# A Strassen-type matrix product whose shared products are handed from PSUM bank to PSUM bank

## The chip, the core and the metric

The kernel runs on one core of a Trainium2 chip: TensorE (PE) multiplies matrices into PSUM, VectorE (DVE) and ScalarE (ACT) work on SBUF and PSUM, GpSimd (POOL) does a little, and SyncE (SP) issues the weight transfers. The metric is the device time of one execution in microseconds, as the median of several runs. The profile comes from one execution more.

## What is computed

One block of a hybrid encoder, fp32, on 256 tokens of width 2048:

```python
def mixer_block(u, w_in, lb, hg_norm_w, rel_bias, w_branch_a, w_branch_b, w_out):
    z = u @ w_in
    hq, hf, hi, hg, aq, ak, av, gates = jnp.split(z, SPLIT_POINTS, axis=-1)
    ...
    o = hgrn2_scan(...)                              # 8 heads, chunks of 64
    y_a = rms_norm(o, hg_norm_w) * silu(hg)
    y_b = chunk_band_attention(aq, ak, av, rel_bias) # 16 heads
    gate_a, gate_b = jnp.split(jax.nn.sigmoid(gates), 2, axis=-1)
    merged = gate_a * (y_a @ w_branch_a) + gate_b * (y_b @ w_branch_b)
    return merged @ w_out

h = x + mixer_block(rms_norm(x, norm_mix_w), ...)
u = rms_norm(h, norm_mlp_w)
h = h + jnp.square(jax.nn.relu(u @ w_up)) @ w_down   # 2048 -> 8192 -> 2048
return rms_norm(h, norm_final_w)
```

`w_in` is 2048 x 11264, its last 4096 columns are the gates.

## The kernel before

**Products in three parts.** Each fp32 operand is split into a high part in the PE's fast fp32 format and the remainder (`split`, L88: a cast on ACT, a subtraction on DVE), and each product is three matmuls, high by high, high by low, low by high (`mm3`, L142). All weights pass through this: a piece is 128 x 1024 (two k-tiles of 512 columns, 512 KB), read by a DMA that SP issues into one of 7 raw buffers, cast on ACT (`wh`, 6 buffers), subtracted on DVE (`wl`, 6 buffers), then used by 12 matmuls of 512 columns, six for each half m of the tokens.

**Order of the stages.** The start and the HGRN2 projections and scan (`hf`, `hq`, `hi`, `hg`), attention (`aq`, `ak`, `av`), the first two column blocks of gate a (`gemm`, L150), then everything else in units of two column blocks (`gemm_s`, L680): ga2, gb0, gb2 (gates), the two branch products (`gemm2`, plain), wo0 and wo2 (output projection), and for each quarter q of the MLP up q0, up q2, dn q0, dn q2. These are 20 units; the very last, dn32, is a plain product by `gemm2`.

**A unit.** Of its 16 k-tiles the k-tiles 0, 1, 4, 5 form a 2 x 2 block problem (halves m of the tokens, halves n of the columns, two blocks of k), done with seven products p1 to p7 instead of eight, six matmuls each. The left operands of four of them are sums of blocks (S5, S2, S4, S7), made once for each left matrix by `combos` (L659): two full sums, four differences and four splits. The right operands are sums of weight pieces, made in place by `add` on DVE (L693). The other twelve pieces are `plain` (L715), 12 matmuls each, so a unit has 7 x 6 + 12 x 12 = 186 matmuls. Four banks c11, c12, c21, c22 collect the outputs. Products that belong to several outputs are copied on ACT from PSUM to SBUF (`copy`, L703: s1 of p1, s5 of p5, s6 of p6, s67 of p6 + p7), combined on DVE after the tenth k-tile (L746 to L748; for units whose result is added to the residual h1, also with h1 by `fold`, L751), and added or subtracted when the banks are evicted on DVE (`evict`, L654). Gates then take a sigmoid on ACT (L582), up units ReLU (L874) and square (L875).

**What sets the order.** The kernel is written as a sequence, and a scheduler places every instruction on its engine's queue; `high_priority` moves instructions ahead. The pools set what a buffer waits for: PSUM has six banks in `ps_k` for units and two in `ps_tp2` for transposes. The sums of x for the gates (`Sx`, L755) are made at the start of ga2, with the highest priority; those for the other stages inside earlier units. Transposes and splits of the finished blocks (`turn`, `turns`) run between products of the following unit (`between`), those of the last up blocks ahead of the down unit (L879).

Of the kernel before, what the change touches and what calls it, by code (L numbers as in the profile page):

```python
# [16 lines left out]
P = 128  # L17
# [33 lines left out]
def tile_hybrid_block(  # L51
# [205 lines left out]
    mask1 = const.tile([P, 64], F32, name="mask1")  # L257
    band(mask1, [[-2, 64]], 1)
    masks = const.tile([P, len(LEVELS), 192], F32, name="masks")
# [4 lines left out]
    reset = const.tile([P, 2 * T], F32, name="reset")  # L264
    nc.gpsimd.memset(reset, 1.0)
    nc.gpsimd.memset(reset.rearrange("p (c t) -> p c t", t=CH)[:, :, 0:1], 0.0)
    hgw = const.tile([P, DK], F32, name="hgw")
# [233 lines left out]
    yb = []  # L501

# [73 lines left out]
    def token(what):  # L576
        return tk.tile([P, NC], F32, name=what, tag="t", bufs=18)
# [6 lines left out]

    ga, gb = [], []
# [68 lines left out]
    def evict(dst, acc, t, op):  # L654
        with tc.high_priority(offset=2000):
            nc.vector.tensor_tensor(dst, acc, t, op=op)
        return dst

    def combos(lhs, what, home):  # L659

        full = []
        for j in range(2):
            f = tk.tile([P, 2, T], F32, name=f"full_{what}{j}", tag="t", bufs=18)
            nc.vector.tensor_tensor(f, lhs[j][:, :2, 0, :].bitcast(F32), lhs[j][:, :2, 1, :].bitcast(F32), op=ALU.add)
            full.append(f)
        a11, a21 = full[0][:, :, :P], full[0][:, :, P:]
        a12, a22 = full[1][:, :, :P], full[1][:, :, P:]
        made = {}
        s = {i: tk.tile([P, 2, P], F32, name=f"s{i}_{what}", tag="t", bufs=18) for i in (5, 2, 4, 7)}
        nc.vector.tensor_tensor(s[5], a21, a22, op=ALU.subtract)  # L670
        nc.vector.tensor_tensor(s[2], s[5], a11, op=ALU.subtract)
        nc.vector.tensor_tensor(s[4], a12, s[2], op=ALU.add)
        nc.vector.tensor_tensor(s[7], a11, a21, op=ALU.subtract)
        for i in (4, 2, 7, 5):
            t = xp.tile([P, 2, 2, P], F32R, name=f"S{i}_{what}", tag=f"S{i}{home}", bufs=1)
            split(t[:, :, 0, :], t[:, :, 1, :], s[i])
            made[i] = t
        return made

    def gemm_s(lhs, S, w, n0, what, kt0=0, between=None, fold=None):  # L680

        n1 = n0 + NC
        c = {}
        B = {}
        for i, (n, k) in {"11": (n0, 0), "22": (n1, 4), "12": (n1, 0), "21": (n0, 4)}.items():
            B[i] = piece(w, n, kt0 + k, f"{what}{i}")

        def add(dst, b):
            with tc.high_priority(offset=2000):
                nc.vector.tensor_tensor(B[dst], B[dst], B[b], op=ALU.add)  # L693

        def product(i, lh, src, n):
            first = i not in c
            if first:
                c[i] = bank(f"{what}c{i}")
            wh, wl = parts(B[src], w, f"{what}{n}")
            for a in range(2):  # L700
                mm3(c[i], *lh(a), wh[:, a], wl[:, a], first and a == 0, False)

        def copy(i, n):  # L703
            t = token(f"{n}_{what}")
            with tc.high_priority(offset=2000):
                nc.scalar.copy(t, c[i])
            return t

        def of(m, jj):
            return lambda k: lhs_of(lhs, k + 4 * jj, m)  # L710

        def comb(i):
            return lambda k: [S[i][:, k, u, :] for u in range(2)]

        def plain(k, n):  # L715
            wh, wl = parts(piece(w, n0 + n * NC, kt0 + k, f"{what}r{n}_{k}"), w, f"{what}r{n}_{k}")
            for m in range(NM):
                for a in range(2):
# [12 lines left out]
        f = copy("21", "s6")  # L731
        product("11", of(0, 1), "21", "p2")
        plain(6, 1)
        product("21", comb(7), "22", "p7")
        e = copy("21", "s67")
        add("21", "11")
        product("21", of(1, 1), "21", "p4")
        if between:
            between()
        for k in (2, 6, *range(8, KD, 2)):  # L740
            for n in range(2):
                if n == 0 or k >= 8:
                    plain(k, n)
            if k == 10:
                with tc.high_priority(offset=2000):
                    nc.vector.tensor_tensor(f, f, s5, op=ALU.subtract)  # L746
# [47 lines left out]
    def h_blocks(n0):  # L794

        for n in (n0, n0 + 1):
            hT.append(new_act(f"h{n}"))
            hi, lo = hT[n][:, :, 0, :], hT[n][:, :, 1, :]
            for m in range(NM):
                t = h1[n][m]  # L800
                tp = transpose4(t, f"h{n}{m}")
                tmp = tk.tile([P, 4, P], F32, name=f"hw_{n}_{m}", tag="t", bufs=18)
# [11 lines left out]
    for n0 in (0, 2):  # L814
# [26 lines left out]
    for qd in range(NQ):  # L841
# [23 lines left out]
        for c in range(0, 4, 2):  # L865
            rs = {}
            for m, n, acc, t, op in gemm_s(hT, Sh, w_up, qd * (FF // NQ) + c * NC, f"up{qd}{c}", between=turns):
                z = acc
                if t is None:
                    t = token(f"r{qd}{c}")  # L870
                else:
                    z = evict(t, acc, t, op)
                with tc.high_priority(offset=2000):
                    nc.scalar.activation(t, z, AF.Relu, scale=rstd2[:, m:m + 1])  # L874
# [8 lines left out]
        for n, m, acc, t, op in down(uT, Su, qd, last):  # L883
            r = h1[n][m]
            evict(r, acc, r if t is None else t, op or ALU.add)
            if not last:
                continue
            nc.scalar.activation(token(f"ysq_{n}_{m}"), r, AF.Square, accum_out=ssq3[:, m, n:n + 1])
            if n < 3:
                nc.vector.tensor_tensor(r, r, wf[:, n * NC:(n + 1) * NC], op=ALU.mult)  # L890
                continue
# [3 lines left out]
            for i in range(4):  # L895
# [7 lines left out]
                (nc.sync if i % 2 else nc.scalar).dma_start(out[m * P:(m + 1) * P, i * NC:(i + 1) * NC], t)  # L903

# [43 lines left out]
```

## Time and profile before

| | |
|---|---|
| median of 3 runs | 1459.68 us (1458.53 to 1459.84) |
| profiled execution | 1457.01 us, span 1455.3 us |
| mean granted TensorE clock | 0.995 |
| HBM read and written | 269.57 MB, 2.10 MB: 187 GB/s over the span |
| weight loads (PEld) | 1185.7 us busy, 81% |

The span is the time between the first and the last instruction. PE matmuls overlap, so the distance between two starts says more than a duration: a matmul of 512 columns has a record of 0.39 us while the next starts after 0.23. The page and the queries list an instruction group by line, engine, operation, output and inputs, with the count, and in brackets the idle time of the engine ahead of it and what ended it. The bracket names the event that came last, not all that was waited for. The granted clock is a share of full speed.

### The profile page before, as it was taken

To read this page: it belongs to the slowest core of one execution; us is meant where nothing else is said; L and a number is where in the kernel's file an instruction comes from. 1 tells how busy PE (TensorE), PEld (TensorE's weight loads), DVE (VectorE), ACT (ScalarE), POOL (GpSimd) and SP (SyncE) were. 2 spreads that over 40 slices of the span, in tenths; PEclk is the share of its full clock that TensorE was granted. 3 is DMA by queue.
4 is the path that set the end of the run, shared out by engine and by line. 5 is a ranking of instruction groups with operands and counts; after the bars stand their busy time and mean duration, and the time that the engine had idled before them with its cause. 6 is when DMAs were issued, how large, how long until landed. Compare 5 with 4: busy or idle time off the path is not lost.

```text
span 1455.3 us, 18340 instructions
## 1 busy us (share of the span) xinstructions
PE 1430.2 (98%) x6738; PEld 1185.7 (81%) x6738; DVE 1095.4 (75%) x1444; ACT 812.8 (56%) x1060; POOL 34.5 (2%) x96
## 2 busy tenths in 40 slices
PE   9999999999998999999999999999999999999997
PEld 8878888888786888888888888888888888888886
DVE  7888987565657775678898878878777887778853
ACT  6855743464545554445556565566555664457642
POOL 2000001010000000010000000000000000000000
PEclk9999999999999999999999999999999999999999
DMA  9644554646456556666555576555666555667561
GB/s 319 228 152 143 165 170 137 192 131 188 139 167 214 193 180 217 191 219 216 182 168 166 195 230 201 193 183 162 198 221 217 192 165 170 212 202 247 180 196 58
DMA packets 106091, 272.89 MB, mean 188 GB/s; under 512 B 8960, under 2 KB 9728, under 8 KB 105616
## 3 DMA queue, kind: packets, MB, share of 16 engines
q1 hardware_dynamic: 103264, 264.80, 55.8%
q0 software_dynamic: 1584, 5.31, 1.4%
q10 hardware_dynamic: 1152, 1.60, 0.3%
q8 instruction: 53, 0.87, 0.2%
q14 instruction: 38, 0.31, 0.1%
HBM read 269.57 MB, written 2.10 MB: 187 GB/s over the span
## 4 chain that ended last, share of the span: by engine, by line
PE 90%; DVE 3%; DMA 2%; ACT 2%; issue 1%; POOL 0%; SPq 0%; POOLq 0%; ACTq 0%; DVEq 0%
PE acc_ak L171 2%; PE acc_aq L171 2%; PE acc_hq L171 2%; PE ps L395 1%; PE acc_hf L171 1%; PE acc_ba L145 1%; PE acc_bb L145 1%; PE acc_bb L144 1%; PE acc_av L143 1%; PE acc_av L145 1%; PE acc_ba L144 1%; PE acc_bb L143 1%; PE acc_ba L143 1%; PE acc_av L144 1%; PE acc_up22c L143 1%
## 5 line engine op out<-in xcount | busy, mean ns | idle before, releaser
L171 PE MATMUL acc_hf<-act_x,wh_hf 128*128 128x512 f32 x128 | 47.6, 407 | 0.4 <-DVE f L179 0.4
L171 PE MATMUL acc_aq<-act_x,wh_aq 128*128 128x512 f32 x128 | 47.8, 407 | 0.0
L171 PE MATMUL acc_hq<-act_x,wh_hq 128*128 128x512 f32 x128 | 45.6, 396 | 0.0
L171 PE MATMUL acc_ak<-act_x,wh_ak 128*128 128x512 f32 x128 | 45.0, 397 | 0.0
L693 DVE TENSOR_TENSOR raw_up<-raw_up,raw_up 128x1024 f32<-128x1024 f32 x32 | 39.2, 1225 | 1.1
L170 PE MATMUL acc_aq<-act_x,wl_aq 128*128 128x256 f32 x120 | 35.1, 293 | 0.0
L693 DVE TENSOR_TENSOR raw_dn<-raw_dn,raw_dn 128x1024 f32<-128x1024 f32 x28 | 34.3, 1225 | 1.0
L170 PE MATMUL acc_hf<-act_x,wl_hf 128*128 128x256 f32 x120 | 34.4, 287 | 0.1
L90 DVE TENSOR_TENSOR wl_ga<-raw_ga,wh_ga 128x1024 fp32r<-128x1024 f32 x16 | 19.6, 1224 | 19.5 <-ACT wh_ga L89 19.5
L170 PE MATMUL acc_hq<-act_x,wl_hq 128*128 128x256 f32 x120 | 33.6, 280 | 0.0
L170 PE MATMUL acc_ak<-act_x,wl_ak 128*128 128x256 f32 x120 | 33.6, 280 | 0.0
L90 DVE TENSOR_TENSOR wl_av<-raw_av,wh_av 128x1024 fp32r<-128x1024 f32 x16 | 19.6, 1224 | 18.1 <-ACT wh_av L89 18.1
L90 DVE TENSOR_TENSOR wl_dn<-raw_dn,wh_dn 128x1024 fp32r<-128x1024 f32 x16 | 19.6, 1224 | 16.9 <-ACT wh_dn L89 16.9
L90 DVE TENSOR_TENSOR wl_ba<-raw_ba,wh_ba 128x1024 fp32r<-128x1024 f32 x16 | 19.6, 1225 | 16.3 <-ACT wh_ba L89 16.3
L89 ACT CAST wh_ba<-raw_ba 128x1024 fp32r<-128x1024 f32 x16 | 16.9, 1053 | 24.8 <-PE acc_ba L145 10.0
L90 DVE TENSOR_TENSOR wl_bb<-raw_bb,wh_bb 128x1024 fp32r<-128x1024 f32 x16 | 19.6, 1224 | 13.8 <-ACT wh_bb L89 13.8
L90 DVE TENSOR_TENSOR wl_ak<-raw_ak,wh_ak 128x1024 fp32r<-128x1024 f32 x16 | 19.6, 1224 | 13.7 <-ACT wh_ak L89 13.7
L89 ACT CAST wh_bb<-raw_bb 128x1024 fp32r<-128x1024 f32 x16 | 16.9, 1054 | 23.0 <-PE acc_ba L145 11.7
L89 ACT CAST wh_dn<-raw_dn 128x1024 fp32r<-128x1024 f32 x16 | 16.9, 1054 | 23.0 <-PE acc_dn L145 13.3
L89 ACT CAST wh_av<-raw_av 128x1024 fp32r<-128x1024 f32 x16 | 16.8, 1053 | 22.0 <-PE acc_av L145 12.4
L89 ACT CAST wh_aq<-raw_aq 128x1024 fp32r<-128x1024 f32 x16 | 16.8, 1050 | 21.5 <-PE acc_aq L171 8.1
L171 PEld LDWEIGHTS acc_hf<-act_x,wh_hf 128*128 128x128 f32 x128 | 24.2, 189 | 5.5 <-DVE f L179 0.7
(845 smaller groups left out, 5100.4 us busy)
## 6 DMA issues: line engine op xcount, KB each, us to landing
raw_dn<-in_w_down_dram SPq DMA_DIRECT2D x44, 512.0 KB, 4.5
raw_up<-in_w_up_dram SPq DMA_DIRECT2D x32, 512.0 KB, 5.0
raw_ga<-in_w_in_t_dram SPq DMA_DIRECT2D x20, 512.0 KB, 4.5
raw_hi<-in_w_in_n_dram SPq DMA_DIRECT2D x16, 512.0 KB, 4.5
raw_hg<-in_w_in_n_dram SPq DMA_DIRECT2D x16, 512.0 KB, 3.7
raw_aq<-in_w_in_t_dram SPq DMA_DIRECT2D x16, 512.0 KB, 4.6
raw_ak<-in_w_in_t_dram SPq DMA_DIRECT2D x16, 512.0 KB, 3.8
raw_av<-in_w_in_n_dram SPq DMA_DIRECT2D x16, 512.0 KB, 4.3
```

The costliest lines, as they stand in the source:

```text
L89: (copy or nc.scalar.copy)(hi, src)
L90: nc.vector.tensor_tensor(lo, src, hi.bitcast(F32), op=ALU.subtract)
L143: nc.tensor.matmul(acc, hi, wh, start=first, stop=False, skip_group_check=True)
L144: nc.tensor.matmul(acc, hi, wl, start=False, stop=False, skip_group_check=True)
L145: nc.tensor.matmul(acc, lo, wh, start=False, stop=last, skip_group_check=True)
L170: nc.tensor.matmul(acc[:, cb, 0:T], wl[:, c], r[:, 0, :], start=False, stop=False)
L171: nc.tensor.matmul(acc[:, cb, :], wh[:, c], r.rearrange("p u t -> p (u t)"), start=kt == 0, stop=kt == nkt - 1)
L395: nc.tensor.matmul(ps[:, m, :], klf[:, a * P:(a + 1) * P], qrf[:, a * 192:(a + 1) * 192], start=True, stop=True)
L693: nc.vector.tensor_tensor(B[dst], B[dst], B[b], op=ALU.add)
```

## The change

The unit's schedule of products is another. p1 is copied on ACT from bank c11 into bank c21, and p6 and later p7 accumulate on that copy. After p6 the bank is copied to SBUF as u1; `less` (DVE) writes c12 = c22 − u1, c22 holding p5, and p3 and the plain pieces add onto it. After p7 it is copied as u2, and `less` writes c22 = c22 − u2. All four banks then hold their outputs at the end, so no combining and no folding is left: `done` is called for each bank when it is complete, ReLU and sigmoid read PSUM, and h1 takes one addition per bank as before. The first three banks that are written by ACT or DVE get one matmul of values that are overwritten (`fresh`).

The last plain piece of column half n1 with the two `done` calls after it is kept in `late` and stands in the next unit, between p5 and p6 (`flush`). The sums of x are made in the attention stage, their tiles in the pool `tk`. The transposes ahead of a down unit now stand inside it (`between=turns`). The masks, the reset row and `hgw` move to the pool `hp` (the first of these lines is shown). In the whole program PE gets 3 matmuls more, DVE 80 TENSOR_TENSOR fewer, ACT 20 copies fewer; the DMAs are the same in number.

```diff
@@ -254,17 +254,17 @@
-    mask1 = const.tile([P, 64], F32, name="mask1")
+    mask1 = hp.tile([P, 64], F32, name="mask1")
...
@@ -582,6 +583,28 @@
+    def combos(lhs, what, home):
+        full = []
+        for j in range(2):
+            f = tk.tile([P, 2, T], F32, name=f"full_{what}{j}", tag="t", bufs=TOK)
+            nc.vector.tensor_tensor(f, lhs[j][:, :2, 0, :].bitcast(F32), lhs[j][:, :2, 1, :].bitcast(F32), op=ALU.add)
+            full.append(f)
...
+        for i in (4, 2, 7, 5):
+            t = (tk if home == "a" else xp).tile([P, 2, 2, P], F32R, name=f"S{i}_{what}", tag=f"S{i}{home}", bufs=1)
+            split(t[:, :, 0, :], t[:, :, 1, :], s[i])
+            made[i] = t
+        return made
+    Sx = combos(xT, "x", "a")
     ga, gb = [], []
     for n in range(2):
         acc = gemm(xT, w_in_t, C_GA + n * NC, KD, f"ga{n}", wide=True)
@@ -651,33 +674,11 @@
-    def evict(dst, acc, t, op):
+    def evict(dst, acc):
         with tc.high_priority(offset=2000):
-            nc.vector.tensor_tensor(dst, acc, t, op=op)
+            nc.vector.tensor_tensor(dst, acc, dst, op=ALU.add)
-        return dst
-    def combos(lhs, what, home):
...
-            t = xp.tile([P, 2, 2, P], F32R, name=f"S{i}_{what}", tag=f"S{i}{home}", bufs=1)
...
-    def gemm_s(lhs, S, w, n0, what, kt0=0, between=None, fold=None):
+    def gemm_s(lhs, S, w, n0, what, done, kt0=0, between=None, fresh=()):
@@ -693,18 +694,17 @@
-            first = i not in c
-            if first:
-                c[i] = bank(f"{what}c{i}")
             wh, wl = parts(B[src], w, f"{what}{n}")
-            for a in range(2):
-                mm3(c[i], *lh(a), wh[:, a], wl[:, a], first and a == 0, False)
-        def copy(i, n):
-            t = token(f"{n}_{what}")
-            with tc.high_priority(offset=2000):
-                nc.scalar.copy(t, c[i])
-            return t
+            def mm():
+                first = i not in c
+                if first:
+                    c[i] = bank(f"{what}c{i}")
+                for a in range(2):
+                    mm3(c[i], *lh(a), wh[:, a], wl[:, a], first and a == 0, False)
+            return mm
         def of(m, jj):
             return lambda k: lhs_of(lhs, k + 4 * jj, m)
@@ -714,54 +714,94 @@
         def plain(k, n):
             wh, wl = parts(piece(w, n0 + n * NC, kt0 + k, f"{what}r{n}_{k}"), w, f"{what}r{n}_{k}")
-            for m in range(NM):
+            def mm(m):
                 for a in range(2):
                     mm3(c["12"[m] + "12"[n]], *lhs_of(lhs, k + a, m), wh[:, a], wl[:, a], False, k + a == KD - 1)
-        product("11", of(0, 0), "11", "p1")
-        s1 = copy("11", "s1")
-        product("12", comb(4), "22", "p3")
+            return mm
+        def copy(dst, i):
+            with tc.high_priority(offset=2000):
+                nc.scalar.copy(dst, c[i])
+            return dst
+        def seeded(i):
+            c[i] = bank(f"{what}c{i}")
+            if i in fresh:
+                nc.tensor.matmul(c[i], lhs[0][:, 0, 0, 0:P], lhs[0][:, 0].rearrange("p u t -> p (u t)"), start=True, stop=False, skip_group_check=True)
+        def less(dst, i, t):
+            with tc.high_priority(offset=2000):
+                nc.vector.tensor_tensor(c[dst], c[i], t, op=ALU.subtract)
+        p1 = product("11", of(0, 0), "11", "p1")
+        p3 = product("12", comb(4), "22", "p3")
         add("22", "12")
         add("12", "11")
-        product("22", comb(5), "12", "p5")
-        s5 = copy("22", "s5")
-        plain(2, 1)
+        p1()
+        seeded("21")
+        copy(c["21"], "11")
+        product("22", comb(5), "12", "p5")()
+        flush()
         add("11", "22")
-        product("21", comb(2), "11", "p6")
-        f = copy("21", "s6")
-        product("11", of(0, 1), "21", "p2")
-        plain(6, 1)
-        product("21", comb(7), "22", "p7")
-        e = copy("21", "s67")
+        product("21", comb(2), "11", "p6")()
+        u1 = copy(token(f"u1_{what}"), "21")
+        seeded("12")
+        less("12", "22", u1)
+        product("11", of(0, 1), "21", "p2")()
+        ps = plain(2, 0)
+        ps(0)
+        p3()
+        product("21", comb(7), "22", "p7")()
         add("21", "11")
-        product("21", of(1, 1), "21", "p4")
+        u2 = copy(token(f"u2_{what}"), "21")
+        pq = plain(2, 1)
+        pq(0)
+        pq(1)
+        product("21", of(1, 1), "21", "p4")()
+        less("22", "22", u2)
+        ps(1)
         if between:
             between()
-        for k in (2, 6, *range(8, KD, 2)):
-            for n in range(2):
-                if n == 0 or k >= 8:
-                    plain(k, n)
-            if k == 10:
-                with tc.high_priority(offset=2000):
-                    nc.vector.tensor_tensor(f, f, s5, op=ALU.subtract)
-                    nc.vector.tensor_tensor(f, f, s1, op=ALU.add)
-                    nc.vector.tensor_tensor(e, e, s1, op=ALU.add)
-                    if fold:
-                        for m, n, t, op in ((1, 0, s1, ALU.add), (0, 1, f, ALU.subtract), (1, 1, e, ALU.subtract)):
-                            nc.vector.tensor_tensor(t, t, fold(m, n), op=op)
-        return [(0, 0, c["11"], None, None), (1, 0, c["21"], s1, ALU.add), (0, 1, c["12"], f, ALU.subtract), (1, 1, c["22"], e, ALU.subtract)]
-    with tc.high_priority(offset=4000):
-        Sx = combos(xT, "x", "a")
-    for gates, c, col, what in ((ga, 2, C_GA, "ga"), (gb, 0, C_GB, "gb"), (gb, 2, C_GB, "gb")):
+        def both(n, *ks):
+            for k in ks:
+                ps = plain(k, n)
+                ps(0)
+                ps(1)
+        def end(n):
+            for m in range(NM):
+                done(m, n, c["12"[m] + "12"[n]])
+        both(0, 6, 8)
+        both(1, 6, 8)
+        both(0, 10, 12, 14)
+        end(0)
+        both(1, 10, 12)
+        def rest():
+            both(1, 14)
+            end(1)
+        late.append(rest)
+    late = []
+    def flush():
+        while late:
+            late.pop()()
+    for gates, c, col, what, fresh in ((ga, 2, C_GA, "ga", ("21", "12")), (gb, 0, C_GB, "gb", ("21",)), (gb, 2, C_GB, "gb", ())):
         gates += [[None] * NM for _ in range(2)]
-        for m, n, acc, t, op in gemm_s(xT, Sx, w_in_t, col + c * NC, f"{what}{c}"):
-            z = acc
-            if t is None:
-                t = token(f"gate_{what}{c + n}{m}")
-            else:
-                z = evict(t, acc, t, op)
-            gates[c + n][m] = sigmoid(t, z, m)
+        def done(m, n, acc, gates=gates, c=c, what=what):
+            gates[c + n][m] = sigmoid(token(f"gate_{what}{c + n}{m}"), acc, m)
+        gemm_s(xT, Sx, w_in_t, col + c * NC, f"{what}{c}", done, fresh=fresh)
+    flush()
     mT = []
@@ -817,21 +857,8 @@
-        for m, n, acc, t, op in gemm_s(mT, Sm, w_out, n0 * NC, f"wo{n0}", fold=lambda m, n: h1[n0 + n][m],
-                                       between=lambda: h_blocks(0) if n0 else turn(3)):
-            r = h1[n0 + n][m]
-            evict(r, acc, r if t is None else t, op or ALU.add)
-    def down(uT, Su, qd, last):
-        for n0 in (0, 2):
-            if last and n0:
-                for n in (2, 3):
-                    acc = gemm2(uT, w_down, n * NC, KD, f"dn{qd}{n}", kt0=qd * KD, tail=8 if n == 3 else 0)
-                    for m in range(NM):
-                        yield n, m, acc[m], None, None
-                continue
-            for m, n, acc, t, op in gemm_s(uT, Su, w_down, n0 * NC, f"dn{qd}{n0}", kt0=qd * KD, fold=lambda m, n: h1[n0 + n][m]):
-                yield n0 + n, m, acc, t, op
+        gemm_s(mT, Sm, w_out, n0 * NC, f"wo{n0}", lambda m, n, acc, n0=n0: evict(h1[n0 + n][m], acc),
+               between=lambda: h_blocks(0) if n0 else turn(3))
@@ -864,31 +891,30 @@
-            for m, n, acc, t, op in gemm_s(hT, Sh, w_up, qd * (FF // NQ) + c * NC, f"up{qd}{c}", between=turns):
-                z = acc
-                if t is None:
-                    t = token(f"r{qd}{c}")
-                else:
-                    z = evict(t, acc, t, op)
+            def done(m, n, acc, c=c, rs=rs):
+                t = token(f"r{qd}{c}")
                 with tc.high_priority(offset=2000):
-                    nc.scalar.activation(t, z, AF.Relu, scale=rstd2[:, m:m + 1])
+                    nc.scalar.activation(t, acc, AF.Relu, scale=rstd2[:, m:m + 1])
                 nc.scalar.activation(t, t, AF.Square)
                 rs[m, n] = t
-            for n in range(2):
-                pend.append((c + n, [rs[m, n] for m in range(NM)]))
-        turns()
+                if m == NM - 1:
+                    pend.append((c + n, [rs[i, n] for i in range(NM)]))
+            gemm_s(hT, Sh, w_up, qd * (FF // NQ) + c * NC, f"up{qd}{c}", done, between=turns)
...
-        for n, m, acc, t, op in down(uT, Su, qd, last):
+        def out_of(m, n, acc, last=last):
             r = h1[n][m]
-            evict(r, acc, r if t is None else t, op or ALU.add)
+            evict(r, acc)
             if not last:
-                continue
+                return
             nc.scalar.activation(token(f"ysq_{n}_{m}"), r, AF.Square, accum_out=ssq3[:, m, n:n + 1])
             if n < 3:
                 nc.vector.tensor_tensor(r, r, wf[:, n * NC:(n + 1) * NC], op=ALU.mult)
-                continue
+                return
...
@@ -901,6 +927,16 @@
+        for n0 in (0, 2):
+            if not (last and n0):
+                gemm_s(uT, Su, w_down, n0 * NC, f"dn{qd}{n0}", lambda m, n, acc, n0=n0: out_of(m, n0 + n, acc), kt0=qd * KD,
+                       between=None if n0 else turns)
+                continue
+            flush()
+            for n in (2, 3):
+                for m, acc in enumerate(gemm2(uT, w_down, n * NC, KD, f"dn{qd}{n}", kt0=qd * KD, tail=8 if n == 3 else 0)):
+                    out_of(m, n, acc)
```

More of the change, by code (lines that the diff above doesn't have):

```diff
@@ L256, in tile_hybrid_block @@
     LEVELS = (2, 8, 32)
-    mask1 = const.tile([P, 64], F32, name="mask1")
+    mask1 = hp.tile([P, 64], F32, name="mask1")
     band(mask1, [[-2, 64]], 1)
-    masks = const.tile([P, len(LEVELS), 192], F32, name="masks")
+    masks = hp.tile([P, len(LEVELS), 192], F32, name="masks")
     for i, B in enumerate(LEVELS):
@@ L263, in tile_hybrid_block @@
             band(v[:, :, k0:k1, :], [[-4 * B, 32 // B], [-B, k1 - k0], [0, B]], B)
-    reset = const.tile([P, 2 * T], F32, name="reset")
+    reset = hp.tile([P, 2 * T], F32, name="reset")
     nc.gpsimd.memset(reset, 1.0)
     nc.gpsimd.memset(reset.rearrange("p (c t) -> p c t", t=CH)[:, :, 0:1], 0.0)
-    hgw = const.tile([P, DK], F32, name="hgw")
+    hgw = hp.tile([P, DK], F32, name="hgw")
     nc.gpsimd.dma_start(hgw, bass.AP(tensor=hg_norm_w.tensor, offset=hg_norm_w.offset, ap=[[0, P], [1, DK]]))
@@ L501, in tile_hybrid_block @@
     yb = []
+    TOK = 18
     def qk_chunk(col, what, factor, acc=None):
@@ L576, in token @@
     def token(what):
-        return tk.tile([P, NC], F32, name=what, tag="t", bufs=18)
+        return tk.tile([P, NC], F32, name=what, tag="t", bufs=TOK)
     def sigmoid(gate, acc, m):
@@ L583, in sigmoid @@
         return gate
+    def combos(lhs, what, home):
[4 more added lines that the diff above has]
+            full.append(f)
+        a11, a21 = full[0][:, :, :P], full[0][:, :, P:]
+        a12, a22 = full[1][:, :, :P], full[1][:, :, P:]
+        made = {}
+        s = {i: tk.tile([P, 2, P], F32, name=f"s{i}_{what}", tag="t", bufs=TOK) for i in (5, 2, 4, 7)}
+        nc.vector.tensor_tensor(s[5], a21, a22, op=ALU.subtract)
+        nc.vector.tensor_tensor(s[2], s[5], a11, op=ALU.subtract)
+        nc.vector.tensor_tensor(s[4], a12, s[2], op=ALU.add)
+        nc.vector.tensor_tensor(s[7], a11, a21, op=ALU.subtract)
+        for i in (4, 2, 7, 5):
[4 more added lines that the diff above has]
+    Sx = combos(xT, "x", "a")
     ga, gb = [], []
@@ L652, in gemm2 @@
         return acc
-    def evict(dst, acc, t, op):
+    def evict(dst, acc):
         with tc.high_priority(offset=2000):
-            nc.vector.tensor_tensor(dst, acc, t, op=op)
-        return dst
-    def combos(lhs, what, home):
[L661 to L674, printed above, removed]
-            t = xp.tile([P, 2, 2, P], F32R, name=f"S{i}_{what}", tag=f"S{i}{home}", bufs=1)
-            split(t[:, :, 0, :], t[:, :, 1, :], s[i])
-            made[i] = t
-        return made
-    def gemm_s(lhs, S, w, n0, what, kt0=0, between=None, fold=None):
+            nc.vector.tensor_tensor(dst, acc, dst, op=ALU.add)
+    def gemm_s(lhs, S, w, n0, what, done, kt0=0, between=None, fresh=()):
         n1 = n0 + NC
@@ L801, in h_blocks @@
                 tp = transpose4(t, f"h{n}{m}")
-                tmp = tk.tile([P, 4, P], F32, name=f"hw_{n}_{m}", tag="t", bufs=18)
+                tmp = tk.tile([P, 4, P], F32, name=f"hw_{n}_{m}", tag="t", bufs=TOK)
                 nc.vector.tensor_tensor(tmp, tp, bc(wmlp[:, 4 * n:4 * n + 4], 2, P), op=ALU.mult)
```

## Prediction

> **What bounds the kernel now.** The page first: which engine fills the span, and what the chain that ended last is made of.
>
> ```profile
> span 1455.3 us, 18340 instructions
> ...
> PE 1430.2 (98%) x6738; PEld 1185.7 (81%) x6738; DVE 1095.4 (75%) x1444; ACT 812.8 (56%) x1060; POOL 34.5 (2%) x96
> ...
> PEclk9999999999999999999999999999999999999999
> ...
> PE 90%; DVE 3%; DMA 2%; ACT 2%; issue 1%; POOL 0%; SPq 0%; POOLq 0%; ACTq 0%; DVEq 0%
> ```
>
> TensorE is busy for 98% of the span at almost its full clock and carries 90% of the chain. So a change gains only if it takes matmuls away or closes the few gaps between them; work taken off DVE (75%) or ACT (56%) is worth nothing where PE does not wait for it. Where PE waits is in the view of waits, and where it does not is in the table by stretches of time:
>
> ```profile
> PE acc_ga2c L143 <- ACT s_ga L706: 5.7, 1, 5.7
> PE ps L395 <- DVE sd L357: 3.3, 3, 2.9
> ```
>
> ```profile
> core 0: us, PE busy (x) PEld busy (x) DVE busy (x) ACT busy (x) POOL busy (x), PEclk, DMA share, GB/s
> 430.00:453.00 23.00, 17.09 (x67) 13.29 (x66) 18.91 (x24) 12.48 (x17) 0.00 (x0) 0.85 0.37 124
> 900.00:1100.00 200.00, 199.92 (x896) 164.82 (x895) 157.85 (x162) 111.49 (x132) 0.00 (x0) 1.00 0.58 192
> 1100.00:1300.00 200.00, 199.92 (x896) 164.66 (x895) 158.13 (x160) 115.92 (x137) 0.00 (x0) 1.00 0.61 202
> ```
>
> One wait of 5.7 us stands out, at the start of the first product unit (ga2, 430 to 453). In the 400 us of the MLP PE idles 0.16 us in all. So nothing can be won in the 20 units themselves, and much can be lost there; the gain, if any, is in that one gap. Its single instructions (start, duration, engine, line; in brackets the idle time before it and its releaser):
>
> ```profile
> 437.48 0.39 PE L145 MATMUL acc_ga2c<-wh_ga2p,act_x 128*128 128x512 f32 x1
> 443.55 0.80 PE L143 MATMUL acc_ga2c<-wh_ga2p,act_x 128*128 128x512 f32 x1 [5.67 <-ACT s_ga L706]
> 445.43 0.80 PE L145 MATMUL acc_ga2c<-wh_ga2p,S_x 128*128 128x512 f32 x1 [0.24 <-DVE S_x L90]
> 447.71 0.39 PE L144 MATMUL acc_ga2c<-wl_ga2p,S_x 128*128 128x512 f32 x1
> ```
>
> The clock in the same place, and in the other place where PE waited long (us, PE busy, granted clock, DMA share, GB/s):
>
> ```profile
> 443.50:448.00 4.50, 4.22 (x10) 0.54 0.05 17
> ```
>
> ```profile
> 82.00:85.00 3.00, 3.00 (x11) 0.57 0.55 175
> ```
>
> Idle times of 5.67 and of 2.9 us were each followed by a clock near 0.55 for some microseconds. The pace of a warm stretch comes from two first matmuls of neighbouring units, with 186 matmuls of 512 columns between them and no transposes:
>
> ```profile
> 897.45 0.44 PE L143 MATMUL acc_dn02c<-wh_dn02p,act_u 128*128 128x512 f32 x1
> ```
>
> ```profile
> 939.68 0.43 PE L143 MATMUL acc_up10c<-wh_up10p,act_h 128*128 128x512 f32 x1
> ```
>
> 42.23 / 186 = 0.227 us. From 437.48 to 447.71 there are nine intervals, 2.04 us at that pace; they took 10.23. **The transition loses 8.2 us**: 5.67 + 0.24 idle, 2.3 by the cold clock.
>
> What the wait consists of stands in the queues of DVE and ACT (same columns):
>
> ```profile
> 438.34 1.29 DVE L664 TENSOR_TENSOR full_x<-act_x 128x512 f32<-128x512 f32 x2
> 441.01 1.22 DVE L90 TENSOR_TENSOR wl_ga2p<-raw_ga,wh_ga2p 128x1024 fp32r<-128x1024 f32 x1
> 442.15 0.42 DVE L671 TENSOR_TENSOR s_x<-s_x,full_x 128x256 f32<-128x256 f32 x1
> 444.96 0.75 DVE L90 TENSOR_TENSOR S_x<-s_x,S_x 128x256 fp32r<-128x256 f32 x2
> ```
>
> ```profile
> 436.11 1.06 ACT L89 CAST wh_ga2p<-raw_ga 128x1024 fp32r<-128x1024 f32 x1 [3.94 <-DVE raw_ga L693]
> 437.06 1.25 ACT L582 ACTIVATE gate_ga<-acc_ga,rstd 128x512 f32<-128x512 f32 x2
> 439.15 1.99 ACT L89 CAST wh_ga2p<-raw_ga 128x1024 fp32r<-128x1024 f32 x2
> 442.91 0.58 ACT L706 COPY s_ga<-acc_ga2c 128x512 f32<-128x512 f32 x1
> ```
>
> The sums of x stand between the weight splits on DVE, their casts stand ahead of the copy s_ga on ACT, and PE, whose next product needs the bank after that copy, waits for the lot.
>
> **The change part by part.** Durations of what it touches (mean of one in the page's groups; minimum, median and maximum in the others):
>
> ```profile
> L693 DVE TENSOR_TENSOR raw_up<-raw_up,raw_up 128x1024 f32<-128x1024 f32 x32 | 39.2, 1225 | 1.1
> ...
> L90 DVE TENSOR_TENSOR wl_dn<-raw_dn,wh_dn 128x1024 fp32r<-128x1024 f32 x16 | 19.6, 1224 | 16.9 <-ACT wh_dn L89 16.9
> ...
> L89 ACT CAST wh_dn<-raw_dn 128x1024 fp32r<-128x1024 f32 x16 | 16.9, 1054 | 23.0 <-PE acc_dn L145 13.3
> ```
>
> ```profile
> L656 DVE TENSOR_TENSOR s_up<-acc_up10c,s_up x3: 681/683/686, 965.4 to 968.0; 128x512 f32<-128x512 f32 x3
> L706 ACT COPY s_up<-acc_up10c x4: 589/589/590, 926.7 to 939.0; 128x512 f32<-128x512 f32 x4
> L746 DVE TENSOR_TENSOR s_up<-s_up,s_up x8: 684/685/687, 759.2 to 1323.2; 128x512 f32<-128x512 f32 x8
> L874 ACT ACTIVATE r<-acc_up10c,rstd x1: 684/684/684, 963.9 to 963.9; 128x512 f32<-128x512 f32 x1
> ```
>
> Back to back, the queues run a little closer than these durations: the split at 441.01 is followed 1.14 later, the casts at 439.15 take 1.99 / 2, so about 0.95 each, the gates 1.25 / 2.
>
> *Sums of x moved into attention.* They take the 8.2 us away from the gates: −8.2. Where they go they cost DVE 1.29 for the two full sums, eight operations of 0.42, so 4.7 us, and ACT four casts of about 0.41, 1.6 us. Attention has room for it:
>
> ```profile
> 330.00:350.00 20.00, 20.00 (x116) 17.39 (x115) 11.33 (x12) 8.42 (x10) 0.00 (x0) 1.00 0.62 185
> 350.00:370.00 20.00, 20.00 (x95) 16.75 (x94) 10.61 (x10) 7.86 (x8) 0.00 (x0) 1.00 0.61 196
> ```
>
> DVE is free for about 9 of 20 us and ACT for 12, and PE is full. Cost 0; without that cover 6.3.
>
> *What remains at the gates.* p1's first matmul is T = 0 (436.35, five intervals ahead of 437.48). In the order as built, ACT does the cast for p5 (to T = 0.7 as now), two gates (to 1.9), the casts for p6 and p7 (0.95 each, to 3.75), and only then the copy of p1's bank into c21 (to 4.4). DVE finishes its three adds at 0.85 and the split for p5 at 2.1; PE's eighth place is 1.8, so p5 waits 0.3. p6 has the fifteenth place, 14 × 0.227 + 0.3 = 3.5, and waits for the copy until 4.4: 0.9. Together 1.2 with the close spacing and 1.6 with full durations; I take +1.4. So the wait on s_ga becomes a shorter wait on the copy into c21; behind it on PE all the rest queues, and behind the copy on ACT the cast of the next piece, which is not needed for 7 us.
>
> *Three dummy matmuls* (`fresh`): 3 × 0.227 = +0.7, on PE's path.
>
> *Four DVE operations and one ACT copy fewer in each unit.* The three combines go, with them three folds of h1 or three evictions, and two `less` come; four copies become three. 4 × 0.69 and 0.59 us leave queues that PE does not wait for: 0. It matters only as cover.
>
> *The new waits in a unit.* Now p6 waits for the copy into c21, p3 for `less` of c12, the later group of c22 for the second `less`. Postponing the last piece of column n1 (12 matmuls, 2.7 us) gives the first of them cover: the copy can start at 1.6 and end at 2.2, p6 has place 24, T = 5.4. The second `less` has two groups ahead of its user. The tight one is p3. It has place 42, T = 9.5. In a unit after an up unit or a gate (evicted on ACT), ACT waits for place 17 of the late piece (end 4.3), then ReLU 0.68 to 5.0, square to 5.6, ReLU (place 23, end 5.7) to 6.4, cast of r1_2 to 7.35, copy u1 to 7.95; DVE splits r1_2 to 8.55 and `less` ends at 9.2 to 9.3: 0.2 to 0.3 before its turn. In a unit after a down unit or wo (evicted on DVE), DVE has from 1.25 the split of p2, an add, the split of r0_2, an eviction, the split of r1_2, an eviction, the split of p4, `less`: 7.4 to 7.7 by spacing, 8.3 by full durations, so 8.6 to 9.55. `less` is priced at 0.69: the trace has no operation that writes PSUM from DVE. Nearest rows: 0.683 with PSUM read (L656), 0.685 without (L746). Bounds: 0.59 (the ACT copy) below, 1.22 (twice the elements) above; I take the row nearest in shape. At 1.22 p3 would come 0.3 late in each of 18 units (all but ga2 and wo0): 5.4 to 6.3 us. The copy into PSUM likewise, 0.59; even 1.05 has cover. In two units (up10, dn20) the cast for p7 stands behind p3 and costs 0.1 to 0.2 each. For scatter against such margins I allow 0.04 in each of 18 units: +1.0 together, between 0 and 6.3.
>
> On this price a rule speaks against the change: the Trainium skill's Perfetto Trace Analysis, Optimizing Scalar/DVE Operations, gives DVE a larger access overhead on PSUM (about 125 ns) than on SBUF (about 60), ScalarE the reverse. As an estimate from that page, a `less` with PSUM at both ends would take some 0.07 to 0.13 longer, and p3 would still be in time or 0.1 late in the tightest units, 0 to 2 us in all. This trace does not bear the overhead out on the reading side: 0.683 against 0.685.
>
> *Other edits.* The masks in another pool and the token count move no instruction of note. The transposes that stood between up and down now stand inside the down unit: as many as before. DMAs: 518 on SP in both. The postponed piece's transfer goes out behind the next unit's four blocks, into the buffer of the piece seven before it, whose split is done some three pieces of 2.7 us ahead of the unit's end; its cast is due at T = 2. That is about 10 us, for a transfer of
>
> ```profile
> raw_up<-in_w_up_dram SPq DMA_DIRECT2D x32, 512.0 KB, 5.0
> ```
>
> 5.0 us. Cost 0, hidden by PE's work on those pieces; later by 5 us it would hold up the late piece.
>
> **Sum**: −8.2 + 1.4 + 0.7 + 1.0 = −5.1 us, a span of 1450.2. The profiled execution took 1457.01, 1.7 over its span, and the median shown is 2.7 above it: 1459.68 − 5.1 = **1454.6 us**, 0.35% faster.
>
> **The rivals.**
> *A: `less` is late at p3 (slower).* One piece more ahead of it on DVE than the walk has (1.14), as when ACT hands over r1_2 one cast late. Ready at 10.4 instead of 9.25, PE waits 0.9 in 18 units, 16 us: 1470. Against a gain of 6.1 without the allowance it decides from 0.34 us per unit on, and is slower by over 0.2% from 0.5. For it: margins of 0.2 in queues full to 75%, and that PE has no slack anywhere. Against it: an average DVE load that falls, and an order that is known.
> *B: the clock still falls at the gates.* 2.9 us of idle did it, 1.4 lies below; nothing here shows from where it starts. If it does, 2.3 come back: −2.8, 1456.9, within 0.2%.
> The Trainium skill, TensorE: Matmul & The Clock Gate, Part 1, puts it at an idle window of about 3.4 us that runs freely; by that rule B does not happen. The trace agrees only roughly, as 2.9 us sufficed.
> *C: the sums are not hidden in attention.* Then it does not do what it says, it only moves them: up to 6.3 come back, +1.2 at worst, 1460.9. Against it: PE at 20.00 of 20 with both engines half idle.
> *D: nothing remains at the gates and in the units*: −8.2 + 0.7, 1452.2.
>
> **How the numbers follow.** Forecast 0.56, A 0.2, B 0.12, C 0.06, D 0.06. About 0.2% (2.9 us) is what a measurement of this kernel can tell from no change. Faster: the forecast less 0.02 (its allowance at the high end), and D: 0.6. Same: B, C and that 0.02: 0.2. Slower: A, 0.2. The forecast's own range is 1452.2 to 1457.5. For 8 in 10 it reaches down to 1451, a little past D, and up to 1463, past C and the bound of `less` (1459.9), into the mild part of A.
>
> **What would show it.** After: the wait of acc_ga2c on s_ga gone and one of 1 to 1.5 us on the copy into c21 in its place, granted clock there near 1; unit to unit 42.2 to 42.3 us in the MLP. A is right if the view of waits lists PE on DVE's `less` for the c12 banks with 18 or so entries of some tenths of a microsecond; B if the clock after the gates is near 0.55; C if attention is longer up to ga0. A total of such waits over 5 us would make the prediction wrong.

## The result and the profile after

The changed kernel takes **1450.28 us** (median of 4 runs, 1447.38 to 1451.27) against 1459.45 before: ratio 0.9935, 95% interval 0.9918 to 0.9952. A second series on another chip gave 1450.16 against 1459.18, ratio 0.9946 (0.9933 to 0.9960). So it is about 0.6% faster, 9 us by the medians. The forecast was 1454.6 in a range from 1451 to 1463: the sign is right, the gain nearly twice as large, and the time lies just below the range.

The page of the profiled execution (1450.73 us), and its list of PE's waits (total, times, longest):

```profile
span 1449.0 us, 18212 instructions
...
PE 1427.1 (98%) x6741; PEld 1185.2 (82%) x6741; DVE 1047.8 (72%) x1364; ACT 807.3 (56%) x1040; POOL 34.5 (2%) x96
```

```profile
PE ps L395 <- DVE sd L357: 3.3, 3, 2.9
PE acc_dn02c L143 <- ACT wh_dn02r L89: 1.8, 1, 1.8
PE acc_hf L174 <- DVE wl_hf L90: 1.5, 1, 1.5
...
PE acc_ga2c L143 <- ACT acc_ga2c L726: 0.6, 1, 0.6
...
PE acc_dn20c L143 <- ACT act_u L89: 0.5, 1, 0.5
PE acc_ga2c L144 <- DVE wl_ga2p L90: 0.2, 1, 0.2
```

The wait on s_ga is gone; 0.6 and 0.2 stand in its place. New is a wait of 1.8 us in dn02 on a cast, and one of 0.5 in dn20, neither of them foreseen. The 1.5 us of hf lie at the start, ahead of the part that is compared below, and differ from trace to trace (1.1 in the second one of the changed kernel, 0.2 in the second one of before). `less` doesn't appear. The gates, in stretches of all engines (columns as in the table before) and in single matmuls:

```profile
430.00:453.00 23.00, 22.24 (x97) 17.75 (x96) 19.99 (x18) 14.31 (x18) 0.00 (x0) 1.00 0.61 206
```

```profile
436.91 0.39 PE L143 MATMUL acc_ga2c<-wh_ga2p,act_x 128*128 128x512 f32 x1
...
439.04 0.50 PE L144 MATMUL acc_ga2c<-wl_ga2p,S_x 128*128 128x512 f32 x1 [0.15 <-DVE wl_ga2p L90]
...
441.31 0.50 PE L143 MATMUL acc_ga2c<-wh_ga2p,S_x 128*128 128x512 f32 x1 [0.60 <-ACT acc_ga2c L726]
```

```profile
438.77 2.00 ACT L89 CAST wh_ga2p<-raw_ga 128x1024 fp32r<-128x1024 f32 x2
440.67 0.59 ACT L726 COPY acc_ga2c<-acc_ga2c 128x512 f32<-128x512 f32 x1
```

PE is busy for 22.24 of 23 us instead of 17.09, at full clock; p6 comes at 441.31, 4.4 us after p1's first matmul, behind the copy that ends 441.26, the place and the price of the forecast. `less` and p3 in up12 (DVE and PE timelines):

```profile
967.20 0.69 DVE L737 TENSOR_TENSOR acc_up12c<-acc_up12c,u_up 128x512 f32<-128x512 f32 x1
```

```profile
968.27 0.39 PE L143 MATMUL acc_up12c<-wh_up12p,S_h 128*128 128x512 f32 x1
```

It ends at 967.89, 0.38 us ahead; in the 19 units behind ga2 it is 0.38 to 0.62 in every one.

**Where the time went.** One number of every trace separates the change from what comes before it: from the first matmul of ga2 (its start in PE's timeline) to the end of the span.

| kernel | from ga2 to the end, us | ga2 to gb0 | p1 of dn02 to p1 of up10 |
|---|---|---|---|
| before, two traces | 1018.95, 1020.61 | 50.44, 50.42 | 42.23, 42.23 |
| changed, two traces | 1012.07, 1012.36 | 41.26, 41.25 | 44.41, 44.55 |

Taken pair by pair, the part from ga2 on is 6.9 and 8.3 us shorter. The changed ga2 has 174 + 2 matmuls up to gb0's p1, as its last piece stands in gb0; at 0.2267 us (42.16 us over 186 in units of the changed kernel without a wait) that is 39.90. So ga2 loses 1.35 us where it lost 8.2: **6.9 us**, the three dummies cost 0.7, and the other 0.7 to 2.1 us come from the rest, though dn02 lost 2.2 us.

### The profile page after: what moved, and what is told of

The parts are those of the page before. It is cut to its first block, busy times and chain, and to the rows that moved or that the text cites. A ratio compares the mean times of both kernels' runs of the same rounds, so it can differ in the third digit from the quotient of the medians.

```text
span 1449.0 us, 18212 instructions
## 1 busy us (share of the span) xinstructions
PE 1427.1 (98%) x6741; PEld 1185.2 (82%) x6741; DVE 1047.8 (72%) x1364; ACT 807.3 (56%) x1040; POOL 34.5 (2%) x96
## 4 chain that ended last, share of the span: by engine, by line
PE 93%; DVE 3%; ACT 2%; issue 1%; DMA 1%; POOL 0%; SPq 0%; POOLq 0%; ACTq 0%
PE acc_hq L171 2%; PE acc_ak L171 2%; PE acc_aq L171 2%; PE acc_hf L171 2%; PE ps L395 1%; PE acc_bb L145 1%; PE acc_bb L143 1%; PE acc_ba L145 1%; PE acc_av L145 1%; PE acc_bb L144 1%; PE acc_ba L144 1%; PE acc_av L143 1%; PE acc_ba L143 1%; PE acc_av L144 1%; PE acc_dn02c L143 1%; PE acc_up22c L143 1%
## 5 line engine op out<-in xcount | busy, mean ns | idle before, releaser
L171 PEld LDWEIGHTS acc_hq<-act_x,wh_hq 128*128 128x128 f32 x128 | 24.3, 190 | 5.4
```

The costliest lines, as they stand in the source:

```text
L171: nc.tensor.matmul(acc[:, cb, :], wh[:, c], r.rearrange("p u t -> p (u t)"), start=kt == 0, stop=kt == nkt - 1)
```

## The experiments

Each is the kernel named with the edit shown; times beside runs of the kernel before on the same chip.

**before_again**: the kernel before, unchanged.

> The kernel before once more, for a second profile and more times. Theory 1 (the gap at the gates is the whole gain, and the profiled execution of before was 2 to 3 us shorter than its other runs for a reason that has nothing to do with the change): the second profile is 1458 to 1460 us long, the gates lose 8 us again, and the extra 2 us lie at other places. Rival (the gap at the gates is longer in the usual execution): the gates lose 10 to 11 us in this profile.

1458.33 us, ratio 0.9998 (0.9989 to 1.0006); the profiled execution 1458.09. The gates lose the same, so the rival falls. The trace has one wait more, 1.4 us in wo2 on s_wo (from its list of waits), that the first trace doesn't have:

```profile
PE acc_wo2c L143 <- ACT s_wo L706: 1.4, 1, 1.4
```

**after_again**: the changed kernel, unchanged.

> The changed kernel once more. Both theories: 1447 to 1452 us. If the waits of 1.8 us at dn02 and of 0.5 to 0.9 us in dn20 belong to the order of the change, they are there again at the same places; if they are chance (a transfer that came late), they are elsewhere or gone.

1450.16 us. The waits in dn02 (2.0) and dn20 (0.7) are there again: they belong to the change.

**x_early**: the kernel before with one part of the change.

```diff
-    mask1 = const.tile([P, 64], F32, name="mask1")
+    mask1 = hp.tile([P, 64], F32, name="mask1")
...
+    Sx = combos(xT, "x", "a")
     ga, gb = [], []
...
-    with tc.high_priority(offset=4000):
-        Sx = combos(xT, "x", "a")
```

> The kernel before with the sums of x made in attention (and the masks in the other pool, which makes the room for it), nothing else of the change. Theory 1: this alone brings the gain: 7 to 9 us faster than before, the wait of 5.7 us on s_ga gone with no more than 0.5 us in its place, granted clock near 1 at the gates; within 1.5 us of the changed kernel. Rival 2 (the new order of products and the postponed piece gain in every unit too): the changed kernel is 2 us or more faster than this one.

1452.21 us, ratio 0.9953 (0.9941 to 0.9966): 7 us. The gates take 43.77 us up to gb0, a loss of 1.5, and what is left of the wait is

```profile
PE acc_up32c L143 <- ACT s_up L707: 1.5, 1, 1.5
PE acc_ga2c L143 <- ACT s_ga L707: 1.1, 1, 1.1
```

1.1 us, more than the 0.5 expected. The changed kernel is 2 us faster than this in the median and 1.9 from ga2 on (1014.12): the two answers are not told apart here.

**x_late**: the changed kernel with the sums of x back at the gates.

```diff
-            t = (tk if home == "a" else xp).tile([P, 2, 2, P], F32R, name=f"S{i}_{what}", tag=f"S{i}{home}", bufs=1)
+            t = xp.tile([P, 2, 2, P], F32R, name=f"S{i}_{what}", tag=f"S{i}{home}", bufs=1)
...
-    Sx = combos(xT, "x", "a")
     ga, gb = [], []
...
+    with tc.high_priority(offset=4000):
+        Sx = combos(xT, "x", "a")
```

> The changed kernel with the sums of x made at the gates with the highest priority, as before. Theory 1: the gap returns, 5 to 8 us slower than the changed kernel, a wait of 4 to 6 us of acc_ga2c and a clock near 0.55 after it. Rival 2: 2 to 4 us slower, and still 4 us or more faster than before.

1451.82 us, 0.9954 (0.9942 to 0.9967), only 1.7 above the changed kernel. The first answer fails, and the second one's price too is a little high. In its timeline and stretches (PE only) at the gates:

```profile
438.94 0.50 PE L143 MATMUL acc_ga2c<-wh_ga2p,act_x 128*128 128x512 f32 x1 [2.65 <-ACT acc_ga2c L725]
```

```profile
438.00:441.00 3.00, 1.95 (x7) 1.00 0.43 162
```

PE waits 2.65 us instead of 5.67 and the clock does not fall. Loss at the gates: 43.30 − 39.90 = 3.4 us. So either half of the change alone takes most of the gap away, the early sums 6.7 of 8.2 us, the new order of products 4.8; both together 6.9. Some 2.3 of the 4.8 are the clock that stayed up, and that is a single trace: of the five runs the profiled one has a mean clock of 0.999, the slowest (1454.21 us) 0.994, like the runs of before.

**no_late**: `late.append(rest)` becomes `rest()`.

> The changed kernel without the postponement: the last piece of column n1 stands at the end of its own unit. Theory 1 (the postponed piece is what keeps p3 clear of the evictions): p3 comes twelve matmuls, 2.7 us, earlier after p1, the queues of DVE and ACT are as long as before, `less` has 0.4 to 0.5 us of slack in the changed kernel, so p3 waits about 2 us in each of 18 units: 20 to 40 us slower than the changed kernel. Rival 2 (the postponement hardly matters, the gain is at the gates): within 3 us of the changed kernel.

1448.64 us, 0.9934 (0.9919 to 0.9949): not slower at all. `less` ends 0.41 to 0.62 us ahead of p3 in the 18 units behind gb0, for the casts and splits of the last piece move ahead with it. Theory 1 falls. The transfers go out in another order there, and the waits in dn02 and dn20 are gone (42.36 us from dn02 to up10).

**less_twice**: the line `less("12", "22", u1)` stands twice.

> The changed kernel with the subtraction that fills c12 done twice in a row (the same values again), one more DVE operation of 0.69 us ahead of p3. In the changed kernel `less` ends 0.38 to 0.49 us ahead of p3's first matmul, of which some 0.07 is handover. Theory 1 (that slack is all there is): p3 waits 0.2 to 0.3 us in 18 units, 3 to 6 us slower than the changed kernel, with entries of acc_..c on that line in the list of waits. Rival 2 (later work makes up for it or the order moves): within 1 us.

1453.09 us, 0.9963 (0.9949 to 0.9977); 1015.77 us from ga2 on, 3.4 to 3.7 more than the changed kernel. The size is the expected one. The list of waits has no entry of p3, and its largest behind ga2 are others:

```profile
PE acc_dn02c L143 <- ACT u_dn L726: 1.4, 1, 1.4
...
PE acc_up10c L144 <- DVE wl_up10r L90: 0.3, 1, 0.3
```

Yet p3 is held up, without idle time. The instruction order has p7 ahead of p3 now, and in up12 p3 starts just behind the end of the second `less`, at 971.60 (DVE, then PE):

```profile
970.91 0.69 DVE L737 TENSOR_TENSOR acc_up12c<-acc_up12c,u_up 128x512 f32<-128x512 f32 x1
```

```profile
971.39 0.39 PE L145 MATMUL acc_up12c<-wh_up12p,S_h 128*128 128x512 f32 x1
971.66 0.50 PE L143 MATMUL acc_up12c<-wh_up12p,S_h 128*128 128x512 f32 x1
972.00 0.39 PE L144 MATMUL acc_up12c<-wl_up12p,S_h 128*128 128x512 f32 x1
```

These starts are 0.27 and 0.34 us apart where the pace is 0.227. In the seven units in which the second `less` ends within 0.02 us of p3's place (gb0, gb2, up02, up12, dn10, up22, up32) the twelve matmuls of p7 and p3 take 0.17 to 0.19 us more, 1.25 together. So the mechanism of the first answer is there, and smaller than it said. Another 1.5 to 1.7 us are lost in dn02 (46.08 us against 44.41 and 44.55), though its waits are shorter than in the changed kernel: behind them the clock fell, which costs about 1.6 us, eight intervals near 0.43 in place of 0.227 (stretch, PE only):

```profile
887.00:890.00 3.00, 3.00 (x9) 0.54 0.76 235
```

The rest is the balance of smaller losses and gains, the largest 0.6 lost in up10 and 0.9 to 1.1 gained in dn20.

**raw8** and **wh7**: what holds dn02 up. In the changed kernel, ACT's and PE's timelines, and SP's:

```profile
879.42 1.05 ACT L89 CAST wh_dn02r<-raw_dn02r 128x1024 fp32r<-128x1024 f32 x1
884.13 2.00 ACT L89 CAST wh_dn02r<-raw_dn02r 128x1024 fp32r<-128x1024 f32 x2 [3.66 <-PE acc_dn02c L144]
```

```profile
886.18 0.50 PE L143 MATMUL acc_dn02c<-wh_dn02r,act_u 128*128 128x512 f32 x1 [1.84 <-ACT wh_dn02r L89]
```

```profile
878.65 0.33 SPq L639 DMA_DIRECT2D raw_dn02r<-in_w_down_dram  x1
```

The casts at 884.13 are those of r0_8 and, behind it, r1_2, which PE needs next. r1_2 had landed at 861.76, but its cast has the buffer that p3 gives back late, and the scheduler put r0_8 ahead of it. r0_8's transfer in turn stands on SP behind those of r1_6, r1_8 and r0_10, though ACT casts it before them: it went out at 878.65 and landed at 884.03. (The bracket names PE, which was done long before; the transfer ended the wait.)

```diff
-    BUFS = {"raw": (6, 1), "wh": (4, 2), "wl": (4, 2)}
+    BUFS = {"raw": (6, 2), "wh": (4, 2), "wl": (4, 2)}   raw8
+    BUFS = {"raw": (6, 1), "wh": (4, 3), "wl": (4, 2)}   wh7
```

> The changed kernel with eight raw buffers for weight pieces instead of seven. Theory 1 (the waits of 2.0 to 2.3 us in dn02 and of 1.5 us in dn20 come from a transfer that was issued late for want of a buffer, in front of which ACT's queue stands): the wait in dn02 falls to 1 us or less; 1 to 3 us faster than the changed kernel. Rival 3 (the order of the casts on ACT alone): dn02 waits 2 us as before, same time within 1 us.

> The changed kernel with seven buffers for the high parts instead of six. In dn02 the cast of r1_2 then stands ahead of that of r0_8 on ACT, as it doesn't have to wait for p3's buffer. Rival 3 (the cast of r1_2, whose piece landed 8 us earlier, is held up by the strict order on ACT behind a cast that waits for its transfer): the wait in dn02 is gone, 2 us or more faster than the changed kernel unless the new order makes `less` late. Theory 1: dn02 still waits 1 us or more.

raw8: **1444.74 us**, 0.9909 (0.9895 to 0.9924), more than the 1 to 3 us expected. wh7: 1445.28, 0.9914 (0.9900 to 0.9929). Each removes the wait in its own way; behind ga2 neither lists any wait of PE up to the last unit. With the eighth buffer ACT goes through the same stretch without a halt for a transfer:

```profile
876.76 2.00 ACT L89 CAST wh_dn02r<-raw_dn02r 128x1024 fp32r<-128x1024 f32 x2
880.36 1.05 ACT L89 CAST wh_dn02r<-raw_dn02r 128x1024 fp32r<-128x1024 f32 x1 [1.60 <-PE acc_dn02c L145]
```

From ga2 on they take 1008.55 and 1009.02, 3.0 to 3.8 us less than the changed kernel: 2.0 to 2.2 in dn02, 1.2 to 1.3 in dn20, 0.3 at the end, beside the second trace of it. So both explanations of the wait hold: it needs the late transfer and the strict order on ACT. The eighth buffer also puts SP's transfers nearer to the order of their use (r1_2, r0_6, r1_6 and both pieces of k = 8 ahead of k = 10); how much of the gain is the buffer and how much that order wasn't tried.

**x_early_raw8, raw8_nolate, raw8_again**: x_early and no_late with the eighth raw buffer, and raw8 once more.

> The kernel before with the sums of x made in attention and eight raw buffers: the old order of products and evictions, beside the new one with as many buffers. If the new order saves in the units once no transfer is late (after the gates the profile of the changed kernel with eight buffers is 5.6 us shorter than that of the old order with the early sums), this one stays 3 us or more slower than that. Rival (the eighth buffer is worth as much to the old order, whose waits of 1.4 to 1.5 us on s_wo and s_up are late transfers too): it gains 2 us or more by the buffer and ends within 3 us of it.

> The changed kernel with eight raw buffers and without the postponed piece. If the postponement is worth nothing, as its removal alone showed (p3 found its bank 0.41 to 0.54 us early then too), this is within 1 us of eight buffers alone. If it is worth something that the late transfers in dn02 and dn20 covered up there, this is 1 to 3 us slower.

> The changed kernel with eight raw buffers once more, on the same chip as the two beside it: 1443 to 1447 us, the waits in dn02 and dn20 again below 0.5 us.

1447.60 (0.9926; 0.9912 to 0.9940), 1446.43 (0.9919; 0.9905 to 0.9932) and 1446.33 us (0.9917; 0.9905 to 0.9930); from ga2 on 1011.21, 1009.80 and 1008.56. The rival of x_early_raw8 holds: the old order gains by the buffer too (2.9 us from ga2 on, 1.7 of them in up32 and 1.25 in wo2), and with equal buffers the new order is 2.65 us shorter in the traces, 1.3 in the medians, which that spread doesn't tell from none. The postponed piece is worth 1.2 us in the traces and nothing that the medians show. raw8 has the lowest median of all, though wh7 is not told from it. It is faster than before in both series, and than the changed kernel by 3.5 us from ga2 on in both traces; by the ratios the two intervals of the changed kernel and those of raw8 touch only between 0.9918 and 0.9930.

## Why the prediction was wrong, step by step

- *The gap at the gates*: right. 8.2 us before in both traces, 1.35 after (forecast 1.4), clock 1.00, the wait on the copy into c21 at T = 4.4. Its ascription was too narrow: I gave it all to the move of the sums, and in x_late the new order alone takes 4.8 of it.
- *Sums hidden in attention*: right. From the first matmul of aq to that of ga2 it takes 220.8 us before and 220.6 after (215.58 to 436.35, 216.28 to 436.91).
- *Three dummies, 0.7*: as counted; not tried by themselves.
- *`less` at p3*: right within 0.2 us. 0.38 to 0.62 of slack where the walk had from 0.05 late to 0.9 early; 0.69 us each, so the row nearest in shape was the price. Rival A falls: not one entry. This trace doesn't bear out the overhead either that the Trainium skill's Perfetto Trace Analysis, Optimizing Scalar/DVE Operations, gives DVE on PSUM: with PSUM at both ends

```profile
L737 DVE TENSOR_TENSOR acc_up12c<-acc_up12c,u_up x2: 692/696/700, 967.2 to 973.9; 128x512 f32<-128x512 f32 x2
L726 ACT COPY u_up<-acc_up12c x2: 590/590/591, 965.9 to 971.2; 128x512 f32<-128x512 f32 x2
```

  0.696 against 0.683 to 0.685, a hundredth, not 0.07 to 0.13.
- *"Nothing can be won in the 20 units themselves", and +1.0 for them*: **the step that failed**, in its sign. In the first pair of traces the units together gain 0.7 us (2.1 in the second, where wo2 of before waits 1.4 more), though dn02 loses 2.2, and up22 and dn20 together 1.1; so the others gain some 4: 0.6 in each of the first two pairs of units with the transposes of an up block (88.68 to 88.10 in the first quarter), 1.0 in the last, 1.2 in wo2, 0.3 in wo0, 0.07 where nothing waits. I argued from the busy share of PE, 199.92 of 200, between 900 and 1300 us. Two things were wrong with that. The 20 units begin at 436, and most of wo2's 1.2 is idle time that stood in the list of waits of before and that I passed over; it is gone after the change, and in the old order with eight buffers too:

```profile
PE tp_h L106 <- DVE hw L803: 0.8, 1, 0.8
```

  The rest leaves no idle time at all, as matmul records of 0.39 us overlap when one starts each 0.227. Here, in up12 of before, the second start is 0.32 behind the first, and no bracket says so:

```profile
987.21 0.48 PE L143 MATMUL acc_up12c<-wh_up12r,act_h 128*128 128x512 f32 x1
987.53 0.39 PE L144 MATMUL acc_up12c<-wl_up12r,act_h 128*128 128x512 f32 x1
```

  Summed over up12 and dn10, start to start, the 32 transposes cost 3.56 us before and 3.30 after, and late starts between matmuls 0.81 and 0.48; PE's idle time there was 0.08. The distance from unit to unit, which I used for the pace only, shows it: 42.23 for 186 matmuls against 42.16 now. Which part of the new order brings these 0.6 us wasn't tried by itself; without the postponed piece (no_late) up12 and dn10 take 88.36, between 88.71 before and 88.12 after.
- *"Cost 0" for transfers and the order of casts*: wrong by 2.2 us in dn02. I counted the lead of the postponed piece, not of the next ones. The order as built has r1_2's cast behind r0_8's in this unit and r0_8's transfer behind three that are used later; the walk followed DVE there, not ACT and SP. That the sum is only 1.2 us off is luck, as this loss and that of up22 and dn20 cancel most of what the other units gain.
- *The offset to the median*: I carried 2.7 us from before to after. In the changed kernel the profiled execution is 0.45 above the median; the offset is chance. These 3 us are the difference between 6.3 us (one profiled execution against the other) and 9.2 (median against median), and with them the forecast misses the result by 4.3 us; the sum itself is 1.2 off, 6.3 against 5.1. Two sources of the scatter show in the traces: the clock below, and single late transfers in the old order. What part of the medians' 9 us each makes up isn't settled.
- *B* fell (clock 1.00 behind 0.6 us of idle time), but less_twice shows that 1.4 us can be followed by the slow clock. *C* fell, and *D*, 1452.2, came nearest, though for other reasons: something did remain at the gates, and the units paid for it.

## What to carry to other kernels

Where one engine's records overlap, measure the lost time from start to start over a known count of instructions, not from its busy share. Where a casting engine works in strict order, look in the built order for casts that wait for a transfer and stand ahead of one that is needed sooner: one more buffer, of 4 KB a partition, was worth 3.5 to 3.8 us from ga2 on, more than the new order of products added to the early sums (1.8 to 2.1). Go through the whole list of waits before saying that nothing waits. And compare traces from a point behind the start, which differed by 3 us between two executions of one kernel (433.69 and 436.91).

## What the runs showed of the hardware that was not expected

The same idle time is followed by the slow clock in one execution and not in the next. PE waits 2.88 to 2.95 us in every trace at about 81 us (L395 on sd). before_again, then after_again (first matmul behind the wait; stretch of 3 us: PE busy, granted clock):

```profile
81.09 0.94 PE L395 MATMUL ps<-qr,kl 128*128 128x192 f32 x4 [2.93 <-DVE sd L357]
```

```profile
82.00:85.00 3.00, 3.00 (x10) 0.50 0.46 160
```

```profile
80.56 0.89 PE L395 MATMUL ps<-qr,kl 128*128 128x192 f32 x4 [2.94 <-DVE sd L357]
```

```profile
82.00:85.00 3.00, 3.00 (x19) 1.00 0.27 107
```

In 7 of the 13 traces the clock fell there, and from the first matmul of hg to that of aq those took 138.5 to 140.0 us; in the other 6 it stayed, and they took 136.9 to 137.0. Behind the 5.67 us at the gates it fell in both traces of before; behind the 2.65 us of x_late and the waits of 1.84 to 2.29 us in dn02 (the changed kernel, twice, and x_late) it did not. In less_twice it fell behind 1.42 us and, 0.6 us later, 0.21 more; that is one trace. The Trainium skill, TensorE: Matmul & The Clock Gate, Part 1, says that the window of about 3.4 us runs freely, so that the same kernel has a different number of slow matmuls from run to run. The traces agree on the chance in it. That the clock can fall behind a wait of 2.9 us, and in one trace behind 1.4, is what this case shows.
